# Cumulative sums in split fp32, keys by transposing, and square roots on ScalarE in three norms of a two-layer hybrid model

## The chip, the cores and the metric

One core of a Trainium2 chip runs the whole program. The metric is the device time of one execution in microseconds (us), of which the median over several runs is given. The engines are TensorE (PE in the profile; PEld is its weight load), VectorE (DVE), ScalarE (ACT), GpSimd (POOL) and SyncE (SP), whose queue issues most of the DMA transfers. Each engine works through its own queue in order and waits there on semaphores.

## The reference

The model has 256 tokens of width 1024 and two layers. Each layer is feed-forward, mixer, feed-forward, each with a root-mean-square norm ahead of it and a residual sum behind it; a last norm closes the program. The first layer's mixer joins retention and gated linear attention (GLA); the second one's joins a gated linear recurrence (RG-LRU) and an mLSTM. What the change touches, cut to its core:

```python
def rmsnorm(x, w):
    y = x * lax.rsqrt(jnp.mean(x * x, axis=-1, keepdims=True) + EPS)
    return y * w

# GLA: decay of every key channel, from a rank-16 projection, then sums over chunks of 64 tokens
log_a = jax.nn.log_sigmoid(glr @ w_lr_up + b_lr) / GLA_TAU      # 256x16 @ 16x256
b = jnp.cumsum(gc, axis=3)
b_mid = b[:, :, :, L // 2 - 1:L // 2]
s = einsum('bhnld,bhnsd->bhnls', qc * exp(b - b_mid), kc * exp(b_mid - b))
upd = einsum('bhnsd,bhnsv->nbhdv', kc * exp(b_end - b), vc)

# mLSTM: keys from the convolved and activated input
mc = silu(causal_dwconv(mu, ml_conv_w, ml_conv_b))
q = einsum('bshi,hij->bshj', mc, ml_wq)
k = einsum('bshi,hij->bshj', mc, ml_wk) * (ML_DH ** -0.5)
upd_c = einsum('bhns,bhnsd,bhnsv->nbhdv', w_end, kc, vc)

def swiglu(x, w_gu, w_down):
    g, u = split(x @ w_gu, 2, axis=-1)
    return (silu(g) * u) @ w_down
```

## The kernel before

The 256 tokens are two halves of 128, called t = 0 and t = 1 in the code; a half's tokens are the 128 partitions of a tile. All is fp32. A large product is taken as three products of a faster type (fp32r): `split` (L128) makes a high part (`hi`, ScalarE, L130) and the remainder (`lo`, VectorE, L131) of each operand, and `mm3` (L205) multiplies high by high (L209), low by high (L210) and high by low (L212) into one PSUM tile. A plain fp32 product is one instruction in the code and two on TensorE.

Units of work (a slice of a weight matrix with what is computed from it) are run in order, each for both halves, the second half lagging behind the first. Weights come as `raw` or `draw` tiles by DMA, and are split ahead of use. The feed-forward blocks combine some weight and activation slices by sums first (`draw`, formed on VectorE at L564; products at L547), so that seven products serve in place of eight. The small steps of the mixers (gates, convolutions, scans) run as side chains (`chain`, L186): each of their steps waits a number of ticks given in `STEPS`, and a tick is 512 columns of a large product on TensorE. So a side chain's matmuls fall between large products. Beyond that, a scheduler with a model of each engine orders the instructions of every engine, and `after` and `high_priority` bind some of them.

The places that the change touches:

- **The norms ahead of the feed-forward blocks** (`norm_f`, L332). ScalarE squares a half and sums it (L345, its sum read out behind it); GpSimd adds eps (L347) and raises to -0.5 (L348) to give `rs`; VectorE multiplies the half with the norm's weights (L349, `hs`) and then with `rs` (L352, two halves of 512 columns); TensorE transposes `hs` (L360) and the result is split (`Th`, `Tl`). The norms called f20, f11 and f21, ahead of the first layer's second block, the second layer's first and its second one, go this way; the first block's takes its root elsewhere.
- **GLA** (`gla_chain`, L794). The rank-16 gate input is transposed, multiplied by `w_lr_up` (tile `wlru`, L803), goes through a log-sigmoid (L738) to `la`, and is then summed over the tokens of a chunk in three ways by constant triangular matrices (`cum`, L811 to L813), with two columns of full sums (L815). The exponentials of these scale queries and keys.
- **mLSTM** (`ml_chain`, L1185). TensorE makes queries and keys from `mc` (L1195, L1196), channels on the partitions; ScalarE copies them out as `mqT` (L1199) and, scaled, `mkT` (L1200); TensorE makes the scores (L1204). For the first half the keys are needed once more with tokens on the partitions, for the state's update; TensorE multiplies `mc` by the key weights the other way round for it (L1212), and VectorE scales the result with the gate (L1215). The second half's chain begins with the convolution (ScalarE L1107, VectorE L1111) and a SiLU (L1189) that gives its `mc`.
- **The final norm** (`final_part`, L418). As above, by two halves of 512 columns; VectorE adds the two sums (L433), GpSimd raises to -0.5 (L434), VectorE scales 704 columns (L436) and ScalarE 320 (L437), and SyncE issues two stores (L439).

ScalarE holds one set of function tables at a time; where the next function needs another, an ACT_TABLE_LOAD stands ahead of it in the profile, with that function's line.

## Time and profile before

| | |
|---|---|
| median of 3 runs | 964.65 us (964.14 to 964.99) |
| profiled execution | 964.23 us, of which the span is 962.5 us |
| granted TensorE clock | 0.998 of full speed |
| instructions in the span | 11855 |
| table loads on ScalarE | 28, each 1.28 us |

The span runs from the first instruction to the last. A timeline row gives the start, the duration of the whole row, engine, line, operation, tiles (out<-in), shape, and with xN the number of instructions joined in it; a bracket names the idle time ahead of the row and what ended it. A group of instructions by line gives minimum, median and maximum in ns and the first and last start in us. Matmuls overlap, so their cost is read from one start to the next.

### The profile page before, as it was taken

The page shows a single profiled execution, that of the slowest core. Times are in us where ns is not written, and L with a number is a line of the kernel's source. Part 1 is how long each engine was busy: PE and PEld are TensorE (multiplying, and loading weights), DVE is VectorE, ACT ScalarE, POOL GpSimd, SP SyncE. Part 2 cuts the span into 40 slices and gives each one's busy share as a digit, 9 for nine tenths or more (in the row PEclk, how much of TensorE's full clock was granted, in tenths as well). Part 3 has the DMA queues.
Part 4 walks back from the last instruction along what each step waited for, and adds up shares of the span by engine and source line. Part 5 has one row for each costly group of instructions (what it writes and reads, how often), then busy time and mean ns, then how long its engine had stood idle before and what let it go on. Part 6 is the DMA issues. An engine that isn't in the chain of part 4 may idle for free.

```text
span 962.5 us, 11855 instructions
## 1 busy us (share of the span) xinstructions
PE 947.5 (98%) x4546; PEld 780.9 (81%) x4546; DVE 806.2 (84%) x932; ACT 602.5 (63%) x772; POOL 33.0 (3%) x60
## 2 busy tenths in 40 slices
...
DMA packets 105497, 180.86 MB, mean 188 GB/s; under 512 B 8196, under 2 KB 55200, under 8 KB 105440
## 3 DMA queue, kind: packets, MB, share of 16 engines
...
q8 instruction: 36, 0.59, 0.3%
q10 hardware_dynamic: 432, 0.55, 0.2%
q14 instruction: 21, 0.17, 0.0%
HBM read 179.03 MB, written 1.05 MB: 187 GB/s over the span
## 4 chain that ended last, share of the span: by engine, by line
PE 76%; DVE 11%; ACT 5%; issue 3%; DMA 3%; POOL 1%; SPq 0%; POOLq 0%; ACTq 0%; DVEq 0%
PE ps L547 20%; PE ps L209 9%; PE ps L212 9%; PE ps L210 9%; PE acc L209 8%; PE acc L212 8%; PE acc L210 8%; DVE lo L131 5%; DMA raw<-in_ffn_wgu_dram 2%; ACT hi L130 2%; DVE draw L564 1%; PE ps L574 1%; PE ps L226 1%; DVE mc L1111 1%; DMA draw<-in_ffn_wgu_dram 0%
## 5 line engine op out<-in xcount | busy, mean ns | idle before, releaser
L131 DVE TENSOR_TENSOR lo<-raw,hi 128x512 fp32r<-128x512 f32 (+4 forms) x222 | 301.8, 1382 | 51.8 <-ACT hi L130 51.0
L130 ACT ACTIVATE hi<-raw 128x512 fp32r<-128x512 f32 (+4 forms) x222 | 254.5, 1186 | 50.8 <-PE ps L212 25.5
L209 PE MATMUL ps<-hi,Th 128*128 128x512 f32 (+3 forms) x544 | 211.9, 390 | 0.2 <-ACT hi L130 0.2
L210 PE MATMUL ps<-lo,Th 128*128 128x512 f32 (+3 forms) x544 | 206.0, 379 | 2.2 <-DVE lo L131 2.2
L212 PE MATMUL ps<-hi,Tl 128*128 128x512 f32 (+3 forms) x544 | 205.9, 379 | 0.0
L131 DVE TENSOR_TENSOR lo<-draw,hi 128x2048 fp32r<-128x2048 f32 x72 | 164.1, 2285 | 10.2 <-ACT hi L130 9.8
L130 ACT ACTIVATE hi<-draw 128x2048 fp32r<-128x2048 f32 x72 | 137.8, 1916 | 38.8 <-DVE draw L564 25.7
L209 PE MATMUL acc<-hi,aT 128*128 128x512 f32 x352 | 138.9, 395 | 0.0
L210 PE MATMUL acc<-lo,aT 128*128 128x512 f32 x352 | 137.0, 390 | 0.0
L210 PEld LDWEIGHTS ps<-lo,Th 128*128 128x128 f32 x544 | 102.5, 188 | 21.2 <-DVE lo L131 4.2
L212 PEld LDWEIGHTS ps<-hi,Tl 128*128 128x128 f32 x544 | 102.2, 188 | 19.0
L209 PEld LDWEIGHTS ps<-hi,Th 128*128 128x128 f32 x544 | 102.2, 188 | 18.9 <-issue 1.4
L212 PE MATMUL acc<-hi,aT 128*128 128x512 f32 x352 | 109.6, 390 | 0.0
L564 DVE TENSOR_TENSOR draw<-draw,draw 128x2048 f32<-128x2048 f32 x36 | 81.9, 2283 | 3.8 <-DVE lo L131 2.7
L130 ACT ACTIVATE aT<-ps 128x256 fp32r<-128x256 f32 x88 | 32.8, 379 | 78.3 <-PE ps L226 51.2
L212 PEld LDWEIGHTS acc<-hi,aT 128*128 128x128 f32 x352 | 66.1, 188 | 13.9
L209 PEld LDWEIGHTS acc<-hi,aT 128*128 128x128 f32 x352 | 66.1, 188 | 13.1
L210 PEld LDWEIGHTS acc<-lo,aT 128*128 128x128 f32 x352 | 66.2, 188 | 13.0
L547 PE MATMUL ps<-hi,Th 128*128 128x512 f32 x144 | 57.0, 396 | 0.4 <-ACT hi L130 0.3
L547 PE MATMUL ps<-lo,Th 128*128 128x512 f32 x144 | 56.2, 390 | 0.8 <-DVE lo L131 0.8
L547 PE MATMUL ps<-hi,Tl 128*128 128x512 f32 x144 | 56.2, 390 | 0.0
L131 DVE TENSOR_TENSOR aT<-ps,aT 128x256 fp32r<-128x256 f32 x88 | 36.4, 418 | 18.8 <-ACT aT L130 18.6
...
## 6 DMA issues: line engine op xcount, KB each, us to landing
...
```

The costliest lines, as they stand in the source:

```text
L130: S.activation(hi2, src2, AF.Copy)
L131: V.tensor_tensor(out=lo2, in0=src2, in1=hi2.bitcast(F32), op=ALU.subtract)
L209: T.matmul(ps, xh[:, k, :], wk[0][:, sl], start=start, stop=False)
L210: T.matmul(ps, xh[:, k, :], wk[1][:, sl], start=False, stop=False)
L212: state["mm"] = T.matmul(ps, xl[:, k, :], wk[0][:, sl], start=False, stop=stop)
L226: T.transpose(pt[:, i * P:(i + 1) * P], src[:, i * P:(i + 1) * P], ident)
L547: state["mm"] = T.matmul(ps, x[a][:, k, :], w[b][:, k, :], start=first and k == 0 and i == 0, stop=k == 3 and i == 2, skip_group_check=not ...
L564: state["dve"] = V.tensor_tensor(out=out, in0=a, in1=b, op=op)
L574: T.transpose(pt[:, i * P:(i + 1) * P], a[:, i * P:(i + 1) * P], ident)
L1111: V.scalar_tensor_tensor(out=dst[:, g, :], in0=cb[:, g, o - 3 + i:o - 3 + i + P], scalar=cw[:, g, i:i + 1], in1=dst[:, g, :], op0=ALU.mult ...
```

## The change

- GLA: `w_lr_up` and the transposed gate are split, and their product becomes three fp32r products. `la` is split, and each of the three cumulative sums becomes two fp32r products, since the entries of the constant matrices are exact in fp32r; the two columns of full sums stay fp32. The constants come in two transfers, and ScalarE copies the larger. One entry of `STEPS`, the delay ahead of the sums, goes from 5 to 8.
- mLSTM, first half: the keys with tokens on the partitions come from transposing `mkT`, which is scaled already.
- Norms f20, f11, f21, first half: ScalarE takes the square root of mean plus eps, VectorE the reciprocal. A square root of a constant one into the same tile is placed after the large product last issued, at high priority. Second half: ScalarE adds eps, GpSimd takes the power as before.
- Final norm: ScalarE takes the root of the two sums' total (one sum as its bias), VectorE the reciprocal; the store of 320 columns goes to ScalarE's queue.

```diff
@@ -43,7 +43,7 @@
 TRP = 10
 NT = 2
 NTF = 10
-STEPS = (2, 2, 10, 5, 3, 3, 6, 7, 3, 1, 1, 30, 10, 10, 9, 8, 3, 2, 10, 3, 3, 2, 9, 2)
+STEPS = (2, 2, 10, 8, 3, 3, 6, 7, 3, 1, 1, 30, 10, 10, 9, 8, 3, 2, 10, 3, 3, 2, 9, 2)
 
 CUT = 320
 
@@ -123,6 +123,9 @@
 
     mh4 = cpool.tile([P, 4], F32, tag="mh4", name="mh4")
     G.memset(mh4, -0.5)
+
+    eps = cpool.tile([P, 1], F32, tag="eps", name="eps")
+    G.memset(eps, EPS)
 
 
     def split(src2, hi2, lo2):
@@ -342,10 +345,18 @@
             if not scaled:
                 ms = apool.tile([P, 1], F32, tag="ms", bufs=2, name=nm("ms"))
                 junk = apool.tile([P, D], BF16, tag="junk", bufs=1, name=nm("junk"))
+                rs = apool.tile([P, 1], F32, tag="rs1", bufs=4, name=nm("rs"))
+                if t == 0:
+
+                    with after(state["mm"]):
+                        S.activation(rs, one, AF.Sqrt)
                 S.activation(junk, h[t], AF.Square, scale=D ** -0.5, accum_out=ms)
-                rs = apool.tile([P, 1], F32, tag="rs1", bufs=4, name=nm("rs"))
-                G.tensor_scalar(out=ms, in0=ms, scalar1=EPS, scalar2=None, op0=ALU.add)
-                G.tensor_tensor(out=rs, in0=ms, in1=mh4[:, 0:1], op=ALU.pow)
+                if t == 0:
+                    S.activation(rs, ms, AF.Sqrt, bias=eps, scale=1.0)
+                    V.reciprocal(out=rs, in_=rs)
+                else:
+                    S.activation(ms, ms, AF.Identity, bias=eps, scale=1.0)
+                    G.tensor_tensor(out=rs, in0=ms, in1=mh4[:, 0:1], op=ALU.pow)
             V.tensor_tensor(out=hs, in0=h[t], in1=wB, op=ALU.mult)
             for n in range(2):
                 sl = slice(n * 512, n * 512 + 512)
@@ -430,13 +441,14 @@
             V.tensor_scalar(out=ms[:, 0:1], in0=ms[:, 0:1], scalar1=EPS, scalar2=None, op0=ALU.add)
             return
         rs = mt("frs", [P, 1], 2)
-        V.tensor_tensor(out=ms[:, 1:2], in0=ms[:, 1:2], in1=ms[:, 0:1], op=ALU.add)
-        G.tensor_tensor(out=rs, in0=ms[:, 1:2], in1=mh4[:, 0:1], op=ALU.pow)
+
+        S.activation(rs, ms[:, 1:2], AF.Sqrt, bias=ms[:, 0:1], scale=1.0)
+        V.reciprocal(out=rs, in_=rs)
         a, b = slice(0, CUT), slice(CUT, D)
         V.tensor_scalar(out=o[:, b], in0=hw[:, b], scalar1=rs, scalar2=None, op0=ALU.mult)
         S.activation(o[:, a], hw[:, a], AF.Copy, scale=rs)
-        for x in (b, a):
-            nc.sync.dma_start(out[0, t * P:(t + 1) * P, x], o[:, x])
+        nc.sync.dma_start(out[0, t * P:(t + 1) * P, b], o[:, b])
+        nc.scalar.dma_start(out[0, t * P:(t + 1) * P, a], o[:, a])
 
 
     def ffn_units(wgu, wd, nxt, layer0=False):
@@ -772,9 +784,17 @@
         def pre():
             open_pool("even")
             C["tri"] = const("tri", I["c_tri"], [P, P])
-            C["lrup"] = mconst("wlru", w_lr_up, [16, 256])
+            up = mt("rb", [16, 256])
+            nc.sync.dma_start(up, w_lr_up)
+            C["lrup"] = mt("lruh", [16, 256], 1, F32R), mt("lrul", [16, 256], 1, F32R)
+            split(up, *C["lrup"])
             C["blr"] = mconst("blr", brow(b_lr), [P, 256])
-            C["cum"] = mconst("cum", I["c_cum"], [P, 3 * P + 2])
+            C["cum"] = mconst("cum", I["c_cum"][:, 3 * P:], [P, 2])
+
+            cum = mt("sq", [P, 3 * P], 1)
+            nc.sync.dma_start(cum, I["c_cum"][:, :3 * P])
+            C["cumr"] = mt("cumr", [P, 3 * P], 1, F32R)
+            S.activation(C["cumr"], cum, AF.Copy)
             C["gmask"] = mconst("gmask", I["c_gmask"], [P, 2 * P], I32)
             for t in range(2):
                 load_rope(t, 0)
@@ -796,23 +816,28 @@
             yield STEPS[0]
             pt = ps_tile(tag="acc")
             T.transpose(pt[:16, :P], gl, ident)
-            glT = mt("glT", [16, P])
-            V.tensor_copy(glT, pt[:16, :P])
+            glT = mt("glTh", [16, P], 1, F32R), mt("glTl", [16, P], 1, F32R)
+            split(pt[:16, :P], *glT)
             yield STEPS[1]
             pz = ps_tile(tag="acc")
-            T.matmul(pz[:, :256], glT, C["lrup"], start=True, stop=True)
+            for i, (a, b) in enumerate(((0, 0), (0, 1), (1, 0))):
+                T.matmul(pz[:, :256], glT[a], C["lrup"][b], start=i == 0, stop=i == 2)
             la = mt("gz", [P, 256])
             V.tensor_tensor(out=la, in0=pz[:, :256], in1=C["blr"], op=ALU.add)
             logsigmoid(la, la, "g", 256)
+            lhl = mt("ge", [P, 256], 1, F32R), mt("E4", [P, 256], 1, F32R)
+            split(la, *lhl)
             yield STEPS[2]
 
             pb = ps_tile(tag="acc")
             pe = ps_tile(tag="acc")
-            T.matmul(pb[:, :256], C["cum"][:, 0:P], la, start=True, stop=True)
-            T.matmul(pb[:, 256:], C["cum"][:, P:2 * P], la, start=True, stop=True)
-            T.matmul(pe[:, :256], C["cum"][:, 2 * P:3 * P], la, start=True, stop=True)
+            last = None
+            for n, dst in enumerate((pb[:, :256], pb[:, 256:], pe[:, :256])):
+                for i in range(2):
+                    with after(last):
+                        last = T.matmul(dst, C["cumr"][:, n * P:(n + 1) * P], lhl[i], start=i == 0, stop=i == 1)
             for p in range(2):
-                T.matmul(pe[:, 256 + 2 * p:258 + 2 * p], la[:, p * P:(p + 1) * P], C["cum"][:, 3 * P:3 * P + 2],
+                T.matmul(pe[:, 256 + 2 * p:258 + 2 * p], la[:, p * P:(p + 1) * P], C["cum"],
                          start=True, stop=True)
             E1 = mt("E1", [P, 256])
             E2 = mt("E2", [P, 256])
@@ -1207,13 +1232,11 @@
             Sw = mt("mSw", [P, 4, P], 1)
             V.tensor_tensor(out=f2(Sw), in0=psS, in1=f2(E), op=ALU.mult)
             if t == 0:
-                pk2 = ps_tile(tag="acc")
-                for hd in range(4):
-                    T.matmul(pk2[:, hd * P:(hd + 1) * P], mc[:, hd, :], C["wqk"][:, 1, hd, :], start=True, stop=True)
+                pk2 = transposes(f2(kT), 4)
                 kw = mt("mkw", [P, 4, P])
                 for hd in range(4):
                     V.tensor_scalar(out=kw[:, hd, :], in0=pk2[:, hd * P:(hd + 1) * P], scalar1=E[:, hd, P - 1:P],
-                                    scalar2=sc, op0=ALU.mult, op1=ALU.mult)
+                                    scalar2=None, op0=ALU.mult)
             else:
 
                 yield has(t, "wi")
```

How the order of the instructions changes, at the three places of which the prediction speaks. First TensorE at the cumulative sums of the first half (`gz` is `la`; `ge` and `E_309` are its high and low part). A row of the order is one instruction of the code.

Before:

```order
L811 MATMUL acc_1737<-gz_1644,cum_1376 128x256
L812 MATMUL acc_1737<-gz_1644,cum_1376 128x256
L813 MATMUL acc_1738<-gz_1644,cum_1376 128x256
L815 MATMUL acc_1738<-cum_1376,gz_1644 128x2 x2
L308 MATMUL ps_1754<-ident,h_72 128x128
```

Now:

```order
L838 MATMUL acc_1755<-ge_1665,cumr_1386 128x256
L838 MATMUL acc_1755<-E_309_1666,cumr_1386 128x256
L838 MATMUL acc_1755<-ge_1665,cumr_1386 128x256
L838 MATMUL acc_1755<-E_309_1666,cumr_1386 128x256
L838 MATMUL acc_1756<-ge_1665,cumr_1386 128x256
L838 MATMUL acc_1756<-E_309_1666,cumr_1386 128x256
L840 MATMUL acc_1756<-cum_1382,gz_1658 128x2 x2
L311 MATMUL ps_1775<-ident,h_72 128x128
```

The block stands at the same place, between the same large products and ahead of the second half's transposes.

Second, VectorE at the second half's norm f21, ahead of the last feed-forward block: `h` is the residual stream (the mixer's output is added to it), `lo` the remainders of weights of the next products.

Before:

```order
L131 TENSOR_TENSOR lo_6672<-raw_6668,hi_6671 128x1024
L131 TENSOR_TENSOR lo_6681<-raw_6677,hi_6680 128x1024
L732 TENSOR_TENSOR h_72<-acc_6537,h_72 128x512
L732 TENSOR_TENSOR h_72<-acc_6538,h_72 128x512
L131 TENSOR_TENSOR lo_6681<-raw_6677,hi_6680 128x1024
L349 TENSOR_TENSOR hs_6609<-h_72,wB 128x1024
L131 TENSOR_TENSOR lo_6840<-draw_6837,hi_6839 128x2048
L352 TENSOR_SCALAR hs_6609<-hs_6609,rs_6613 128x512 x2
L564 TENSOR_TENSOR draw_6858<-draw_6858,draw_6837 128x2048
```

Now:

```order
L134 TENSOR_TENSOR lo_6707<-raw_6703,hi_6706 128x1024
L744 TENSOR_TENSOR h_72<-acc_6572,h_72 128x512
L744 TENSOR_TENSOR h_72<-acc_6573,h_72 128x512
L134 TENSOR_TENSOR lo_6716<-raw_6712,hi_6715 128x1024
L360 TENSOR_TENSOR hs_6644<-h_72,wB 128x1024
L134 TENSOR_TENSOR lo_6716<-raw_6712,hi_6715 128x1024
L363 TENSOR_SCALAR hs_6644<-hs_6644,rs_6647 128x512 x2
L134 TENSOR_TENSOR lo_6875<-draw_6872,hi_6874 128x2048
```

The subtraction of 2048 columns has moved from ahead of the scaling (L352, now L363) to behind it, and one of 1024 columns stands in its place. At f20, ahead of the first layer's second block, it is the other way round: a subtraction of 2048 columns now stands ahead of the scaling, and one of 1024 did before.

Third, ScalarE in the odd mixer, at the first half's mLSTM chain.

Before:

```order
L1199 COPY mqT_5790<-acc_5780 128x512
L1200 ACTIVATE mkT_5791<-acc_5781 128x512
L1171 ACT_TABLE_LOAD
L1171 ACTIVATE guard_5807<-acc_5805 128x4
L130 ACTIVATE hi_5910<-raw_5908 128x1024
L1107 ACTIVATE xc_5821<-lrucb_5320,lrucw_5318 128x128 x4
```

Now:

```order
L1224 COPY mqT_5824<-acc_5814 128x512
L352 ACT_TABLE_LOAD
L352 ACTIVATE rs_6564<-one 128x1
L1225 ACTIVATE mkT_5825<-acc_5815 128x512
L1196 ACT_TABLE_LOAD
L1196 ACTIVATE guard_5841<-acc_5839 128x4
L1132 ACTIVATE xc_5855<-lrucb_5354,lrucw_5352 128x128 x4
```

The constant's square root of norm f21, with its table load, has come in between `mqT` and `mkT`, and the weight conversion that stood ahead of `xc` has gone behind it.

## The prediction

> **What bounds the kernel now.** I read the totals first, then the chain that ended last, then the gaps in TensorE's timeline.
>
> ```profile
> PE 947.5 (98%) x4546; PEld 780.9 (81%) x4546; DVE 806.2 (84%) x932; ACT 602.5 (63%) x772; POOL 33.0 (3%) x60
> ```
>
> ```profile
> PE 76%; DVE 11%; ACT 5%; issue 3%; DMA 3%; POOL 1%; SPq 0%; POOLq 0%; ACTq 0%; DVEq 0%
> ```
>
> TensorE is busy nearly throughout, and three quarters of the chain are matmuls. So two things pay: TensorE time removed where it runs without a gap, and a gap closed. Work on VectorE, ScalarE or GpSimd counts only where TensorE waits for it, or after its last matmul. The profiled execution took 964.23 us; the median of the runs is 964.65, 0.42 more. I sum against the first and carry the difference over. This measurement can tell a change from none above about 0.2%, 1.9 us.
>
> **Cumulative sums: -1.14.** TensorE's timeline at the first of the two chains, then the group over both, then short split products elsewhere:
>
> ```profile
> 201.33 0.39 PE L212 MATMUL ps<-hi,Tl 128*128 128x512 f32 x1
> 201.56 0.59 PE L811 MATMUL acc<-gz,cum 128*128 128x256 f32 x2
> ...
> 202.85 0.50 PE L815 MATMUL acc<-cum,gz 128*128 128x2 f32 x4
> ```
>
> ```profile
> L811 PE MATMUL acc<-gz,cum x4: 377/377/378, 201.6 to 226.1; 128*128 128x256 f32 x4
> ```
>
> ```profile
> 194.93 0.28 PE L209 MATMUL ps<-hi,Th 128*128 128x256 f32 x1
> 195.05 0.28 PE L210 MATMUL ps<-lo,Th 128*128 128x256 f32 x1
> ```
>
> I count start to start, since matmuls overlap. Three fp32 products take six instructions and 202.85 - 201.56 = 1.29 us. A split product of 256 columns starts every 0.12, so the six new ones take 0.72. That is 0.57 less, twice 1.14. The matmuls stand back to back there, so it is time of the span. The new split ahead of the sums (a ScalarE and a VectorE instruction) costs TensorE nothing: the delay counter ahead of them goes from 5 to 8 ticks, and a tick is 512 columns of other products. Nor do the two splits of the gate's operands, the constants' extra copy, their two smaller loads on SyncE (issued long before use), and two further table loads that the first early root brings into these chains: TensorE has no gap in this stage that the work of the other engines ends, so they have room. If that cover is gone, the first to wait is the sum itself. Bounds: -0.9 to -1.2.
>
> **Rank-16 product: -0.2.**
>
> ```profile
> 193.84 0.69 PE L803 MATMUL acc<-wlru,glT 16*128 16x256 f32 x2
> 194.47 0.39 PE L209 MATMUL ps<-hi,Th 128*128 128x256 f32 x1
> ```
>
> Two instructions take 0.63 (194.47 - 193.84). No row shows a split product with 16 rows. At the full-height 0.12 each, three take 0.36: 0.27 less. With the extra that these two show over the full-height fp32 ones above (0.63 / 2 = 0.315 against 1.29 / 6 = 0.215, so 0.1 each) they take 0.66: nothing saved. Between 0 and -0.27 I take -0.1 for each of the two chains, nearer the row that has 16 rows.
>
> **Keys: -0.4 of TensorE time.**
>
> ```profile
> 696.80 1.05 PE L1212 MATMUL acc<-wqk,mc 128*128 128x128 f32 x8
> 697.61 0.36 PE L209 MATMUL ps<-hi,Th 128*128 128x256 f32 x1
> ```
>
> ```profile
> 772.21 0.60 PE L360 MATMUL ps<-ident,hs 128*128 128x128 f32 x4
> 772.64 0.38 PE L360 MATMUL acc<-ident,hs 128*128 128x128 f32 x2
> ```
>
> Eight instructions take 0.81; four transposes take 0.43. They now wait for ScalarE's mkT instead of for nothing new; the score product ahead of them in TensorE's queue needs mkT as well, so nothing behind them waits longer. Bounds: -0.4 to 0, if a later wait takes it up.
>
> **Second half's norm ahead of the last feed-forward block: -0.8.** TensorE, VectorE, then GpSimd:
>
> ```profile
> 783.78 0.39 PE L212 MATMUL ps<-hi,Tl 128*128 128x512 f32 x1
> 784.82 0.66 PE L360 MATMUL ps<-ident,hs 128*128 128x128 f32 x4 [0.65 <-DVE hs L352]
> ```
>
> ```profile
> 781.21 2.29 DVE L131 TENSOR_TENSOR lo<-draw,hi 128x2048 fp32r<-128x2048 f32 x1
> ```
>
> ```profile
> 780.57 3.01 POOL L347 TENSOR_SCALAR ms<-ms 128x1 f32<-128x1 f32 x1 [10.53 <-ACT junk L345]
> 783.66 0.58 POOL L348 TENSOR_TENSOR rs<-ms,mh 128x1 f32<-128x1 f32 x1
> ```
>
> A one-column addition takes 3.01 us on GpSimd, and ends 0.08 after VectorE's long subtraction (781.21 + 2.29 = 783.50). The power follows, then the scaling, and TensorE starts 1.04 after its last matmul where 0.23 is usual: 0.81 lost. Afterwards ScalarE adds eps, so one GpSimd step is gone. More important, the order now puts a 1024-column subtraction (1.2 us) there, and the 2048-column one behind the scaling. If the power is shut out until that shorter one ends (781.21 + 1.22 = 782.43), plus 0.43 (next part), the scaling starts near 782.9 and its first half is done near 783.4; TensorE comes for it at 783.78 + 0.23 = 784.01. I take the whole gap, -0.8; the other end is 0.
>
> The Trainium skill, page SBUF — State Buffer, section "SBUF: two separate sides", says that VectorE operations with two SBUF inputs and GpSimd share a port pair as an exclusive lock, held for a whole instruction. The two rows above agree; by it the change gains here through the shorter subtraction and not through the missing addition.
>
> **Second half's norm ahead of the first layer's second block: +0.2.** GpSimd, VectorE, TensorE:
>
> ```profile
> 321.30 1.41 POOL L348 TENSOR_TENSOR rs<-ms,mh 128x1 f32<-128x1 f32 x1
> ```
>
> ```profile
> 321.06 1.22 DVE L131 TENSOR_TENSOR lo<-raw,hi 128x1024 fp32r<-128x1024 f32 x1
> 322.75 0.49 DVE L352 TENSOR_SCALAR hs<-hs,rs 128x512 f32<-128x512 f32 x1 [0.47 <-POOL rs L348]
> ```
>
> ```profile
> 323.74 0.49 PE L360 MATMUL ps<-ident,hs 128*128 128x128 f32 x3
> ```
>
> Here the order changes the wrong way: a 2048-column subtraction (2.29) takes the place of the 1024-column one (1.22) at 321.06 and ends at 323.35. The power ended 0.43 after its subtraction (322.28); shut out again, it ends at 323.78, and the first half of the scaling (0.49) at 324.3. TensorE is there at 323.74 + 0.23 = 323.97, since one matmul moved ahead. So nearly 0.4 is lost, or nothing if the power slips in before the long one. I take 0.2. After the root's table ScalarE must load the SiLU table again, which it didn't here; it has 2.35 us of idle time for it:
>
> ```profile
> 322.57 0.38 ACT L468 ACTIVATE ffs<-ps 128x256 f32<-128x256 f32 x1 [2.35 <-PE ps L212]
> ```
>
> **First half's norms: 0.** ScalarE does one conversion, loads the Sqrt table, takes the root; VectorE inverts:
>
> ```profile
> 308.05 2.01 ACT L130 ACTIVATE hi<-raw 128x1024 fp32r<-128x1024 f32 x2 [0.19 <-PE acc L212]
> ```
>
> ```profile
> 311.95 0.60 PE L360 MATMUL ps<-ident,hs 128*128 128x128 f32 x4
> ```
>
> ```profile
> 705.50 0.30 ACT L743 ACTIVATE fe<-fe,one 128x4 f32<-128x4 f32 x1
> ```
>
> ```profile
> L1254 DVE RECIPROCAL den<-den x4: 156/166/167, 719.7 to 742.8; 128x2 f32<-128x2 f32 x4
> ```
>
> From 308.05: one conversion 1.04, load 1.28 (row below), root 0.30 (a small activation with a bias column), reciprocal 0.17, half a scaling 0.49, and 0.15 of hand-overs: 311.5, and TensorE comes at 311.95. In the last block ScalarE's conversion starts at 768.97:
>
> ```profile
> 768.97 1.99 ACT L130 ACTIVATE hi<-raw 128x1024 fp32r<-128x1024 f32 x2
> ```
>
> The same 3.4 us give 772.4; TensorE came at 772.21, but three matmuls moved ahead, so 772.89. Both have about 0.5 to spare. The third such norm, at the second layer's start, has no conversion ahead of the load and more room. VectorE's reciprocal is a new wait for ScalarE; behind it in its queue stand the scaling and weight subtractions, and a 2.3 us form (L564) was moved out from behind them, so TensorE's next block finds them done. Bounds: 0 to +1.0, if a further conversion of 1.0 slips ahead of each load.
>
> **The early Sqrt in the odd mixer: +0.6.** A root of a constant, which would load the table ahead of the norm at 769, stands between mqT and mkT, some 75 us before it; other functions follow, so the load at the norm remains. The rows there, and the first half's block that waits later:
>
> ```profile
> 692.67 0.60 ACT L1200 ACTIVATE mkT<-acc 128x512 f32<-128x512 f32 x1
> 693.30 1.28 ACT L1171 ACT_TABLE_LOAD   x1
> 694.59 0.17 ACT L1171 ACTIVATE guard<-acc 128x4 f32<-128x4 f32 x1
> 695.61 1.64 ACT L1107 ACTIVATE xc<-lrucb,lrucw 128x128 f32<-128x128 f32 x4
> ```
>
> ```profile
> 715.85 0.49 PE L1195 MATMUL acc<-mc,wqk 128*128 128x128 f32 x2 [0.61 <-ACT mc L1189]
> ```
>
> ScalarE has 1.28 + 0.17 = 1.45 more to do before mkT, and TensorE later waits for ScalarE's mc. Behind mkT stand xc, the gates and mc; VectorE's convolution waits for xc. A conversion of 1.05 that stood before xc now stands behind, so xc is only 0.4 to 0.6 late; but that conversion and its subtraction are then late in turn. On TensorE five more 512-column matmuls (1.1 us) now stand ahead of the block that uses mc, the keys' 0.4 fewer, so it comes there 0.7 later. Ends: -0.6 (the present wait covered) and +1.5 (all 1.45 paid). I take +0.6, as other waits of this stage may grow too.
>
> The Trainium skill, page ScalarE: Activation LUTs, section "What ACT_TABLE_LOAD costs", prices a switch at a 1283 ns load plus a drain of about 1380 ns. This trace has the load but no drain: it starts 0.03 behind mkT's end and the next activation 0.01 behind its own. By the page the sum would be some 3 us worse.
>
> **The end: -0.6.**
>
> ```profile
> 957.41 0.16 DVE L433 TENSOR_TENSOR ms<-ms 128x1 f32<-128x1 f32 x1
> 957.65 0.55 POOL L434 TENSOR_TENSOR frs<-ms,mh 128x1 f32<-128x1 f32 x1 [7.55 <-DVE ms L433]
> 958.23 0.56 ACT L437 ACTIVATE fo<-hw,frs 128x320 f32<-128x320 f32 x1 [0.85 <-POOL frs L434]
> 958.23 0.59 DVE L436 TENSOR_SCALAR fo<-hw,frs 128x704 f32<-128x704 f32 x1 [0.66 <-POOL frs L434]
> 958.82 0.81 SPq L439 DMA_DIRECT2D out_dram<-fo  x2
> ```
>
> Everything here sets the end. Addition and power take 0.82 with their hand-overs (958.23 - 957.41); root 0.30, reciprocal 0.17 and two hand-overs of 0.04 take 0.55: 0.27 less. The two stores were issued one behind the other on SyncE in 0.81; now the second is on ScalarE's queue, so the later starts up to 0.4 earlier. I take -0.6: -0.3 if the second queue brings nothing, -0.7 at most. The Sqrt table was loaded for the first half's root, whose power ran over 7 us earlier (the bracket at 957.65).
>
> **Sum.** -1.14 - 0.2 - 0.4 - 0.8 + 0.2 + 0 + 0.6 - 0.6 = -2.34: 961.9 profiled, **962.3** as a median.
>
> **Rivals.**
> - *The odd mixer takes it back*: the 1.45 on ScalarE reaches mc in full and the keys' 0.4 is only waited longer. Against it, the moved matmuls. +0.9 and +0.4 on the forecast: 963.6. Chance 0.2.
> - *The change doesn't do what it says at the norms*: GpSimd stays shut out in both second halves, the gap at 783.78 remains. For it, the 3.01 and 1.41 us rows. +0.8 + 0.2: 963.3. Chance 0.1.
> - *A table switch costs twice its row*: a drain as long as the load, at the two tight norms (1.28 - 0.5 each) and in the odd mixer (1.28): +2.8, 965.1. Against it, the 0.01 and 0.03 us around the load. Chance 0.05.
> - *Slower, by the early Sqrt in the odd mixer*: ScalarE is 1.45 late and VectorE idles about 1.0 for xc with its subtractions queued behind. It decides from the point where TensorE pays this 2.45 in both halves' chains, not once: 2 x 2.45 - 0.6 = +4.3, with the norms' spare lost a little more: 967. For it, ScalarE runs gapless around that load. Against it, the halves' chains overlap in time, so a delay is paid once. Chance 0.1.
>
> **How the numbers follow.** My forecast has 0.5, and spans 960.6 to 963.0; a larger gain (rank-16 products, stores) another 0.05. Faster means under 962.7: 0.45 of the forecast's 0.5, all of the larger gain, 0.03 of the rivals: 0.53. Slower means over 966.6: 0.1. The same: 0.37. The range takes in the first three rivals, 960.5 to 965.2, and leaves out the slower case and a little below.
>
> **What would show it.** Six sums about 0.12 apart; TensorE's last L360 group 0.23 after its matmul instead of 1.04, with the GpSimd addition's 3.01 gone; no TensorE wait at the first halves' norms; its wait for mc at most 1.5 us; the reciprocal of the last norm 0.35 behind ScalarE's root's start, and two stores that start together. A wait above 2 us for mc, or a new one at 311 or 772, would make me wrong.

## The result and the profile after

| | before | changed kernel |
|---|---|---|
| median (22 runs each, on the same chips) | 964.22 us (963.21 to 965.11) | 965.54 us (964.80 to 969.05) |
| profiled execution, its span | 964.23, 962.5 us | 964.80, 963.0 us |
| table loads on ScalarE | 28 | 39 |

The ratio is 1.0018, with a 95% interval of 1.0012 to 1.0023: 1.3 us slower at the medians, where 2.3 us faster was forecast. 965.54 lies outside the range. It is 0.18%, so by the bound set ahead it counts as no change, though the interval leaves out 1. One execution of e13 below took 3928.8 us and one of e14 5445.07; without these two their medians are 965.48 and 963.03, and differences in the text use those.

The page of the changed kernel, its first line on engines (busy time, share, instructions) and its shares of the chain:

```profile
PE 946.3 (98%) x4544; PEld 779.4 (81%) x4544; DVE 807.7 (84%) x938; ACT 616.6 (64%) x798; POOL 29.2 (3%) x50
```

```profile
PE 77%; DVE 10%; ACT 7%; DMA 3%; issue 2%; POOL 0%; SPq 0%; DVEq 0%; ACTq 0%; POOLq 0%
```

TensorE's busy sum fell by 1.2 us and ScalarE's rose by 14.1, about what the eleven more table loads take (11 x 1.28). On the chain ScalarE's share rose from 5% to 7%, TensorE's from 76% to 77%, and those of VectorE, GpSimd and issue fell by one point each. Where time went is read by cutting the span at the starts of TensorE rows that every version has: the first row of the rank-16 product, of f20's transposes for each half, of the first half's mLSTM queries, of f21's transposes for the second half, and the last matmul. "End" runs from the last matmul's start to the end of the span. Times in us, each from one profiled execution; the experiments below are in the table as well.

| kernel | start | GLA | f20 | to odd mixer | odd mixer | last block | end | span | median |
|---|---|---|---|---|---|---|---|---|---|
| before | 193.84 | 118.10 | 11.79 | 366.69 | 94.38 | 170.63 | 7.01 | 962.46 | 964.22 |
| changed | 192.36 | 118.57 | 12.28 | 366.54 | 95.42 | 170.81 | 7.03 | 963.02 | 965.54 |
| e1_no_early_root | 192.33 | 117.42 | 12.28 | 366.46 | 96.23 | 170.78 | 7.03 | 962.53 | 965.94 |
| e2_gla_only | 193.28 | 117.26 | 11.79 | 366.89 | 95.48 | 170.76 | 7.45 | 962.90 | 964.42 |
| e3_norms_only | 192.80 | 118.14 | 12.29 | 366.35 | 97.68 | 170.81 | 6.97 | 965.04 | 965.43 |
| e4_tail_only | 193.18 | 118.12 | 11.79 | 366.84 | 94.53 | 170.65 | 6.88 | 961.99 | 963.87 |
| e5_gla_one_load | 192.86 | 117.28 | 11.79 | 367.03 | 94.55 | 170.63 | 7.01 | 961.16 | 963.03 |
| e6_norms_no_early | 193.33 | 118.14 | 12.29 | 366.48 | 94.08 | 170.83 | 6.99 | 962.14 | 964.00 |
| e7_norms_second_only | 193.33 | 118.14 | 11.77 | 366.78 | 94.50 | 170.77 | 6.98 | 962.27 | 964.04 |
| e8_keys_only | 192.75 | 118.09 | 11.79 | 367.16 | 96.76 | 170.85 | 7.01 | 964.40 | 967.26 |
| e9_keys_twice | 194.28 | 118.08 | 11.79 | 366.84 | 94.57 | 170.63 | 7.01 | 963.20 | 964.36 |
| e10_keys_later | 192.97 | 118.08 | 11.79 | 367.18 | 94.79 | 172.08 | 7.01 | 963.90 | 964.43 |
| e11_repaired | 194.25 | 117.44 | 12.28 | 366.58 | 94.17 | 170.78 | 6.81 | 962.32 | 963.52 |
| e12_best | 193.76 | 117.36 | 11.77 | 367.14 | 94.63 | 170.80 | 6.68 | 962.14 | 963.18 |
| e13_without_keys | 192.80 | 118.56 | 12.28 | 366.42 | 94.99 | 170.83 | 7.03 | 962.90 | 965.67 |
| e14_gla_root | 193.45 | 117.30 | 11.79 | 366.63 | 95.23 | 170.63 | 6.72 | 961.75 | 963.05 |
| e15_gla_root_last | 193.73 | 117.38 | 11.77 | 367.12 | 93.96 | 170.81 | 6.68 | 961.46 | 962.79 |
| e16_root_f21 | 192.77 | 117.39 | 12.29 | 366.50 | 94.76 | 170.81 | 7.03 | 961.55 | 964.29 |
| e17_root_not_f21 | 192.65 | 118.53 | 12.29 | 366.45 | 94.09 | 170.79 | 7.04 | 961.82 | 965.40 |

The first stage holds nothing that e4, e8, e9 and e10 edit, and yet it takes 192.75 to 194.28 in them and 193.84 before. In e9, as in e11, TensorE's clock fell to half for 3.41 us at 25 us (last section), which is 1.7 of that; the other four still differ by 1.1. So two spans can't be compared to better than that; GLA, f20 and the end can, since they agree to some 0.05 in kernels that leave them alone. The odd mixer's stage too differs between kernels that leave it as it was: 94.38 before, e5 94.55, e14 95.23, and e2 95.48, as much as the changed kernel. Changed less before, without the start: +0.47 in GLA, +0.49 at f20, -0.15, +1.04 in the odd mixer, +0.18, +0.02 at the end; together +2.05 (the medians say +1.32). The profiled execution needn't be a typical one: that of the changed kernel is the fastest of its 22, e17's of its 11, 1.8 below the median.

**GLA: two new waits.** TensorE's waits of the changed kernel between 190 and 310 us (total, times, longest); before, this list is empty:

```profile
PE acc L894 <- DVE gS L882: 0.5, 1, 0.5
PE acc L879 <- DVE gqkT L868: 0.5, 1, 0.5
```

What stands ahead of the second is read in the timelines of ScalarE, VectorE and TensorE of the changed kernel:

```profile
207.33 1.28 ACT L352 ACT_TABLE_LOAD   x1
208.62 0.20 ACT L352 ACTIVATE rs<-one 128x1 f32<-128x1 f32 x1
208.73 0.67 ACT L942 ACTIVATE gv<-ps,rs 128x512 f32<-128x512 f32 x1
209.31 1.14 ACT L133 ACTIVATE hi<-raw 128x512 fp32r<-128x512 f32 x2
```

```profile
209.96 1.29 DVE L134 TENSOR_TENSOR lo<-raw,hi 128x512 fp32r<-128x512 f32 x2 [1.96 <-ACT hi L133]
211.17 0.68 DVE L868 COPY gqkT<-acc 128x512 f32<-128x512 f32 x1
```

```profile
211.91 0.49 PE L879 MATMUL acc<-gqkT 64*128 64x128 f32 x4 [0.50 <-DVE gqkT L868]
```

f20's early root and its table load hold ScalarE from 207.33 to 208.73. The conversion `hi` behind them is late, VectorE idles 1.96 us for it, and the copy of `gqkT`, which needs nothing from ScalarE, stands in VectorE's queue behind the two subtractions that do. TensorE comes for it 0.5 us too early. `gS` stands behind four more such subtractions. It takes two edits together: in e2, with GLA's edits and no early root, the queue has this order but VectorE idles only 0.52 us there; in e3, with the early root alone, the copy stands ahead of the subtractions, as before. Neither kernel has these waits. It was wrong to ask only whether ScalarE has spare time in the stage: the delay passed through a queue to something else.

**Odd mixer.** ScalarE's timeline of the changed kernel, and TensorE's waits between 690 and 790 us:

```profile
692.11 1.28 ACT L352 ACT_TABLE_LOAD   x1
693.40 0.20 ACT L352 ACTIVATE rs<-one 128x1 f32<-128x1 f32 x1
693.51 0.58 ACT L1225 ACTIVATE mkT<-acc 128x512 f32<-128x512 f32 x1
...
695.47 1.64 ACT L1132 ACTIVATE xc<-lrucb,lrucw 128x128 f32<-128x128 f32 x4
```

```profile
PE ps L213 <- DVE lo L134: 1.7, 2, 1.4
PE acc L212 <- ACT Th L133: 0.6, 1, 0.6
```

The stage starts at 690.43 before and 689.76 now. From there, `mkT` is 1.51 late and `xc` 0.53 late (5.18 before, 5.71 now), as forecast. The wait for `mc` is gone, and so is the 0.6 us for `hs`; in their place TensorE waits for weights (`lo`) and, at 765.82, for the high part of the RG-LRU branch's output (`Th`, from `lh`) at the output product. The wait for `lo` is followed up with e16 and e17.

### The profile page after: what moved, and what is told of

The parts are those of the page before. It is cut to its first block, busy times and chain, and to the rows that moved or that the text cites. A ratio compares the mean times of both kernels' runs of the same rounds, so it can differ in the third digit from the quotient of the medians.

```text
span 963.0 us, 11858 instructions
## 1 busy us (share of the span) xinstructions
PE 946.3 (98%) x4544; PEld 779.4 (81%) x4544; DVE 807.7 (84%) x938; ACT 616.6 (64%) x798; POOL 29.2 (3%) x50
## 4 chain that ended last, share of the span: by engine, by line
PE 77%; DVE 10%; ACT 7%; DMA 3%; issue 2%; POOL 0%; SPq 0%; DVEq 0%; ACTq 0%; POOLq 0%
PE ps L559 20%; PE ps L212 9%; PE ps L213 9%; PE ps L215 9%; PE acc L212 8%; PE acc L213 8%; PE acc L215 8%; DVE lo L134 5%; ACT hi L133 3%; DMA raw<-in_ffn_wgu_dram 2%; DVE draw L576 1%; PE ps L586 1%; PE ps L229 1%; DMA r<-mx 1%; ACT Th L243 1%
```

## Experiments: the parts alone

Each experiment was timed in eleven executions (e8 in eight, e13 in twelve) beside the kernel before on the same chip; a ratio is to that.

**e1, the changed kernel without the early root.**

```diff
-                if t == 0:
-                    with after(state["mm"]):
-                        S.activation(rs, one, AF.Sqrt)
```

> The changed kernel without the square root of the constant one in the three norms (a computation whose result is overwritten, so nothing of the output is left out). Theory A, the early root is what takes the savings: in the changed kernel TensorE waits 0.55 us for gqkT and 0.49 us for gS in the GLA chain, behind a table load of 1.28 us that stands there, and the odd mixer is 2.2 us longer. Without it both go: about 3 us less than the changed kernel's 965.5, so 962.0 to 963.0. Rival B, the odd mixer is longer because the keys' transposes and the other edits reorder it: only the GLA waits go, about 1 us, 964.3 to 964.8. Rival C, the Sqrt loads at the norms themselves: no change, 965.5.

Measured: 965.94 against 964.14, ratio 1.0015 (1.0006 to 1.0024), as slow as with the root: as rival C has it, but not for its reason, since the stages moved: GLA fell by 1.15, to 117.42, and the odd mixer rose by 0.8, to 96.23. Something that the early root had hidden came up there: TensorE's waits are of the kinds of e8 (`Th` 1.2, `hi` 0.7, `hm` 0.7, `lo` 0.6; in e8 1.2, 0.7, 0.6 and 1.0).

**e2, GLA's edits alone** (products, splits, two transfers, the delay of 8).

```diff
+            C["cum"] = mconst("cum", I["c_cum"][:, 3 * P:], [P, 2])
+            cum = mt("sq", [P, 3 * P], 1)
+            nc.sync.dma_start(cum, I["c_cum"][:, :3 * P])
...
+                        last = T.matmul(dst, C["cumr"][:, n * P:(n + 1) * P], lhl[i], start=i == 0, stop=i == 1)
```

> The kernel before with the GLA part alone (split rank-16 product, split sums, delay 8 instead of 5). If the matmuls saved are time of the span, as the prediction put it: -1.14 for the sums and -0.2 to -0.3 for the rank-16 product, ratio 0.9984 to 0.9987, about 962.8 against 964.2. If the extra splits on ScalarE and VectorE bring new waits in that stage, or a later stage takes it back: within 0.3 us of the kernel before.

Measured: 964.42 against 964.14, ratio 1.0001 (0.9992 to 1.0010). GLA's stage does gain 0.84, so the sums' gain is real; the end is 0.43 longer, although nothing at the end was edited.

**e3, the three norms alone, with the early root.**

```diff
+                    with after(state["mm"]):
+                        S.activation(rs, one, AF.Sqrt)
...
+                if t == 0:
+                    S.activation(rs, ms, AF.Sqrt, bias=eps, scale=1.0)
+                    V.reciprocal(out=rs, in_=rs)
+                else:
+                    S.activation(ms, ms, AF.Identity, bias=eps, scale=1.0)
```

> The kernel before with the three norms' part alone, the early root included. Theory A (the early root costs about 1 in the GLA chain and up to 2.2 in the odd mixer, the norm of the last block gains 0.8, the one of the first layer's second block loses 0.2 to 0.3): +1.5 to +2.7 us, 965.7 to 966.9. Rival B (the odd mixer's 2.2 come from the keys and the reordering): +0.3 to +0.6, 964.5 to 964.8.

Measured: 965.43 against 964.14, ratio 1.0017 (1.0008 to 1.0025): the norms alone are as slow as the whole change, but not in the same places. GLA's stage is as before (118.14): the root's place does no harm where VectorE keeps the old order.

**e4, the final norm alone.**

```diff
+        S.activation(rs, ms[:, 1:2], AF.Sqrt, bias=ms[:, 0:1], scale=1.0)
+        V.reciprocal(out=rs, in_=rs)
...
+        nc.scalar.dma_start(out[0, t * P:(t + 1) * P, a], o[:, a])
```

> The kernel before with the final norm's part alone. The trace of the changed kernel shows the root and the reciprocal 0.30 us shorter than the addition and the power, the last store landed 0.12 us sooner after the scaling, and then eight waits of SyncE on the DMA queues, 0.06 us each, that come after the landing instead of before it (0.43 us). Theory T, these waits eat the gain: within 0.1 us of the kernel before. The prediction's own: -0.6 us.

Measured: 963.87 against 964.14, ratio 0.9999 (0.9991 to 1.0008). The end is 6.88 for 7.01: -0.13 where -0.6 was forecast.

## Experiments: which piece of each part

**e5, GLA with the constants in one transfer.**

```diff
-            C["cum"] = mconst("cum", I["c_cum"][:, 3 * P:], [P, 2])
-            cum = mt("sq", [P, 3 * P], 1)
-            nc.sync.dma_start(cum, I["c_cum"][:, :3 * P])
+            cum = mt("sq", [P, 3 * P + 2], 1)
+            nc.sync.dma_start(cum, I["c_cum"])
+            C["cum"] = mt("cum", [P, 2], 1)
+            V.tensor_copy(C["cum"], cum[:, 3 * P:])
```

> The GLA part alone, but with its constants in one transfer instead of two (VectorE copies the two fp32 columns out). The GLA part alone was even with the kernel before although its trace is 0.85 us shorter from the rank-16 product to the next norm. Theory L: its one extra transfer turns the round of the eight DMA queues, so that SyncE's end waits begin with the last store's queue and seven more waits (0.44 us) follow the landing; and the gate's round trip through DRAM in the odd mixer eats part of the rest. With one transfer the 0.44 us come back: 963.1 to 963.7, 0.4 to 0.5 under the GLA part alone. Rival: the end waits don't matter, it stays at 964.1 to 964.5.

Measured: 963.03 against 964.31, ratio 0.9991 (0.9982 to 1.0000). GLA keeps its gain (117.28) and the end is back at 7.01. TensorE's timeline at the rank-16 product and the sums:

```profile
192.86 0.39 PE L812 MATMUL acc<-lruh,glTh 16*128 16x256 f32 x1
...
193.42 0.38 PE L209 MATMUL ps<-hi,Th 128*128 128x256 f32 x1
```

```profile
200.50 0.28 PE L826 MATMUL acc<-ge,cumr 128*128 128x256 f32 x1
...
201.25 0.50 PE L828 MATMUL acc<-cum,gz 128*128 128x2 f32 x4
```

Six sums take 0.75 (1.29 before), the product 0.56 (0.63 before): -0.54 and -0.07 per half, -1.22 in all. The stage shows -0.82. Of the rest, 0.18 is a wait for `rk` at 265.44 that wasn't there before; the other 0.2 stands under no wait that the trace tells.

The end is explained by SyncE's waits there, of before and of e2 (total, times, longest):

```profile
SPq L1474 <- DMA out_dram<-fo: 1.5, 2, 0.9
```

```profile
SPq L1487 <- DMA out_dram<-fo: 1.9, 1, 1.9
```

At the end of each of these programs SyncE waits in turn for eight DMA queues, in the same order, some 0.06 us each. Transfers are dealt round the queues, so one transfer more turns the round by one. In the kernel before, the store that lands last is on the queue asked for last: SyncE's last wait ends at 961.57 and it goes on at 961.63. In e2 that store is on the queue asked for first, and seven more waits follow (961.57 to 962.08). The split transfer so costs e2 0.43 us at the far end of the program. In the changed kernel it is SyncE's own store that is asked for first; it lands 0.17 us ahead of ScalarE's, and the seven waits run from 961.70 to 962.20. There the turn costs less: its end is 7.03, with the same two stores it is 6.88 in e4 and 6.81 in e11.

**e6, e3 without the early root** (the same three lines removed as in e1).

> The kernel before with the norms' part alone and without the early root. With the early root it was 1.3 us slower than the kernel before. Theory A': the early root's 1.45 us on ScalarE in the odd mixer are most of it; without it 963.5 to 964.4. Rival B': the first half's roots at the norms reorder the program (the 2048-column subtraction ahead of the scaling at two norms, 0.5 and 0.2 us; other places in the odd mixer): still 965.0 to 966.0, with the trace's waits at f20 and f11 as in the changed kernel.

Measured: 964.00 against 964.31, ratio 0.9995 (0.9986 to 1.0004), 1.6 below e3 (each taken against its own kernel before). The odd mixer's stage is 94.08 against e3's 97.68; the other stages behind the start are equal to 0.2. Of that difference about 1.7 is a fall of TensorE's clock in e3's profiled execution (last section), and 1.9 is left.

**e7, the second halves' norms alone** (the first halves stay on GpSimd).

```diff
+                if t == 0:
+                    G.tensor_scalar(out=ms, in0=ms, scalar1=EPS, scalar2=None, op0=ALU.add)
+                else:
+                    S.activation(ms, ms, AF.Identity, bias=eps, scale=1.0)
```

> The kernel before with only the second half's norms changed (ScalarE adds eps, GpSimd takes the power). The order on VectorE stays that of before, with the 2048-column subtraction ahead of the scaling at the last block's norm. If the port decides, the power is shut out to 783.5 in place of the addition and ends 0.43 later: the scaling starts about 0.3 us sooner, -0.3 us. If the addition was the cost, the whole gap of 0.81 goes: -0.8 us. Rival: no change, under 0.2 us.

Measured: 964.04 against 964.31, ratio 0.9999 (0.9990 to 1.0008). Taking GpSimd's addition away gains nothing in the median. In the trace it gains what the first theory said, 0.3: TensorE starts f21's transposes 0.73 after its last matmul (784.52 after 783.79; 1.04 before), and other small waits of the odd mixer take it up. f20's stage is 11.77: the 0.5 us at f20 comes with the new order of VectorE, which this kernel doesn't have.

**e8, the transposed keys alone.**

```diff
-                pk2 = ps_tile(tag="acc")
-                for hd in range(4):
-                    T.matmul(pk2[:, hd * P:(hd + 1) * P], mc[:, hd, :], C["wqk"][:, 1, hd, :], start=True, stop=True)
+                pk2 = transposes(f2(kT), 4)
```

> The kernel before with the keys' transposes alone. Prediction's step: 0.4 us of TensorE time saved, of the span unless a later wait takes it up. Its order also has a 1024-column subtraction instead of the 2048-column one ahead of the last block's scaling, so if that order gives the 0.8 us and not the norm's change, this kernel gains them too: -0.8 to -1.2 us. If the odd mixer's waits are set by other chains (the gate's round trip through DRAM), the keys' 0.4 are only waited: -0.8 at most, 0 if both fail.

Measured: 967.26 against 964.31, ratio 1.0029 (1.0019 to 1.0039): 3.0 us slower, the most of any kernel here, by an edit that takes 0.4 us off TensorE. TensorE's waits of e8 between 690 and 790 us:

```profile
PE acc L209 <- ACT Th L130: 1.2, 1, 1.2
PE ps L210 <- DVE lo L131: 1.0, 1, 1.0
```

These are its two longest, and none of its waits is for the keys. The scheduler works on modelled times, and with four transposes for eight instructions it arranges the 70 us behind them differently on TensorE, VectorE and ScalarE. VectorE's order just behind (`mSw` and `mkw` are the scores and keys with the gate):

```diff
+L1208 TENSOR_TENSOR mSw_5860<-acc_5849,mE_5803 128x512
+L1213 TENSOR_SCALAR mkw_5867<-acc_5862,mE_5803 128x128 x4
 L741 SCALAR_TENSOR_TENSOR fe_5875<-g_1101_5872 128x4
-L131 TENSOR_TENSOR lo_5919<-raw_5916,hi_5918 128x1024
-L1208 TENSOR_TENSOR mSw_5860<-acc_5849,mE_5803 128x512
-L1215 TENSOR_SCALAR mkw_5867<-acc_5862,mE_5803 128x128 x4
```

The new order also has the 1024-column subtraction ahead of f21's scaling, with GpSimd's addition still there, and TensorE loses nothing at that place:

```profile
786.31 0.40 PE L212 MATMUL ps<-hi,Tl 128*128 128x512 f32 x1
786.54 0.60 PE L360 MATMUL ps<-ident,hs 128*128 128x128 f32 x4
```

**e9, the keys with each transpose done twice**, so that the scheduler sees eight instructions as before.

```diff
-        for i in range(n):
+        for i in [i for i in range(n) for _ in range(rep)]:
...
+                pk2 = transposes(f2(kT), 4, rep=2)
```

> The keys' transposes alone, but each done twice into the same place, so that TensorE works on them about as long (8 of 0.11 us) as on the product that they replace (0.81 us). On VectorE and ScalarE the instructions then stand in the order of before, on TensorE too but for the replaced ones. The keys alone took 3.0 us more than the kernel before, with 4.6 us of TensorE waits in the second half of the odd mixer against 1. Theory O, the new order of the odd mixer costs it, and not the transposes: within 0.3 us of the kernel before, 964.0 to 964.6. Rival D, the new dependence on ScalarE's mkT costs it: still 966 to 967.

Measured: 964.36 against 964.24, ratio 0.9999 (0.9990 to 1.0008). The keys come from the transposes as in e8, the order is that of before, and the 3.0 us are gone: they were the order's, not the transposes'.

**e10, the keys with one delay of the side chains longer**, which nearly restores the order.

```diff
-STEPS = (2, 2, 10, 5, 3, 3, 6, 7, 3, 1, 1, 30, 10, 10, 9, 8, 3, 2, 10, 3, 3, 2, 9, 2)
+STEPS = (2, 2, 10, 5, 3, 3, 6, 7, 3, 1, 1, 30, 10, 10, 9, 8, 3, 2, 10, 4, 3, 2, 9, 2)
```

> The keys' transposes alone, with one delay counter of the mLSTM chain at 4 ticks instead of 3, which brings the order back (all but two instructions on VectorE and ScalarE, 21 on TensorE). Theory O: the waits of the second half go, 964.0 to 964.4, and up to 0.4 less if the TensorE time saved counts, 963.6. Rival D: 966 to 967. If even an order close to the old one is enough to lose, more than 965.

Measured: 964.43 against 964.24, ratio 1.0001 (0.9992 to 1.0010). Without the cost of the order, the keys' 0.4 us still doesn't show. The odd mixer is at 94.79; its profiled execution is 1.4 us longer in the last block and stands 1.3 above its own median. There ScalarE idles 3.81 us, up to 874.42, for a late transfer of down-projection weights (0.88 before), and TensorE then waits 1.28 us at 879.41 for a `cs` that stands in VectorE's queue behind these weights' subtraction.

## Experiments: putting it together

**e11, the changed kernel repaired**: no early root, one transfer, the delay of e10.

> The changed kernel with three repairs: no early root, the sums' constants in one transfer, one delay counter of the mLSTM chain at 4 ticks instead of 3. By the parts: GLA with one transfer -1.3 (measured), norms without the early root -0.3 (measured), final norm -0.1 to -0.3 (measured -0.27 with an interval around 0), keys 0 to -0.4: 962.0 to 962.8, if theory O holds and the parts add up. If the transposes themselves lose, or the parts don't add up, 964 or more.

Measured: 963.52 against 964.24, ratio 0.9990 (0.9981 to 0.9999), 2.0 below the changed kernel.

**e12, the pieces that had gained**: GLA with one transfer, the final root with both stores on SyncE, the keys with the delay of e10, and the new norm at f21 only, without the early root.

```diff
-            norm_f(t)
+            norm_f(t, alt=name == "f21")
...
+        S.activation(rs, ms[:, 1:2], AF.Sqrt, bias=ms[:, 0:1], scale=1.0)
+        V.reciprocal(out=rs, in_=rs)
```

> The GLA part with one transfer, the final norm's root on ScalarE with both stores on SyncE as before, the keys' transposes with the longer delay, and the changed norm at the last block only, without the early root. The norms at f20 and f11, whose order lost 0.5 and 0.2 us, stay as before. By the parts -1.3 (GLA), -0.3 (root), -0.8 (last block's gap), 0 to -0.4 (keys): 961.5 to 962.2. If the odd mixer's waits take it up, 963 or more.

Measured: 963.18 against 964.24, ratio 0.9988 (0.9979 to 0.9997). f20's stage is as before, the end 6.68.

**e13, the changed kernel with the fp32 key product of before.**

```diff
-                pk2 = transposes(f2(kT), 4)
+                pk2 = ps_tile(tag="acc")
+                for hd in range(4):
+                    T.matmul(pk2[:, hd * P:(hd + 1) * P], mc[:, hd, :], C["wqk"][:, 1, hd, :], start=True, stop=True)
```

> The changed kernel without the keys' part (the fp32 product stays), early root and all else as in the change. On ScalarE and VectorE its instructions stand in the changed kernel's order but for one. Theory E, in the changed kernel the early root alone makes the odd mixer longer and the keys change nothing: 965.2 to 966.0. Rival K, the keys' reordering costs in the changed kernel as it does alone: 963 to 964.

Measured: 965.67 against 964.05, ratio 1.0016 (1.0007 to 1.0025), as the changed kernel. With the early root in place the keys neither cost nor gain: the new order of e8 doesn't arise then.

**e14, GLA with one transfer and the final root, stores on SyncE.** The diffs are those of e5 and, of e4, the root without the second queue.

> The GLA part with one transfer and the final norm's root on ScalarE, both stores on SyncE as before; no keys, no other norms. By the parts: 1.3 from GLA and 0.3 from the root, 962.6 to 962.9. If the gain doesn't add up: 963.0 or more.

Measured: 963.05 against 964.05, ratio 0.9989 (0.9980 to 0.9997). The end is 6.72, 0.17 shorter than e4's with its two queues.

**e15, e14 and the new norm at f21 without the early root** (the diff of e12 at `norm_f`).

> As e14, with the last block's norm changed too (first half's root on ScalarE, no early root). The gap of 0.8 us at its second half goes, but the versions e11 and e12 that have this show 1.1 us more of waits at 764 to 766, ahead of it. If those waits come from the changed norm: no gain over e14, within 0.3. If they come from the keys' later delay: 0.8 under e14, 961.8 to 962.1.

Measured: 962.79 against 964.05, ratio 0.9991 (0.9982 to 0.9999). It has the lowest median, and the shortest odd mixer, 93.96. e5, e11, e12, e14 and e15 are all about 0.1% faster than the kernel before (e5's interval ends at 1.0000), and no run here ranks them.

**e16 and e17, the early roots apart**, both on the base of e13. e16 keeps only f21's, e17 only those of f20 and f11.

```diff
-                if t == 0:
+                if t == 0 and early:
...
-            norm_f(t)
+            norm_f(t, early=name == "f21")
```

> The changed kernel with the fp32 key product, in which only norm f21 keeps its early square root of a constant; those of f20 and f11 are gone. The theory that each early root costs where it lands, two times apart: the GLA stage loses its two waits (118.56 to 117.4 us between the rank-16 product and the first half's transposes of f20), while the odd mixer keeps the table load between mqT and mkT, so its stage stays near 95.0 us or above, the SyncE row with the two transfers of the odd mixer's output weights stays 4.2 us long (it is 3.5 in every kernel without this root), and the gate's round trip through DRAM (from GpSimd's store of mx to VectorE's use of mE, second half) stays at 9.4 us. Median about 1.1 below the kernel with all early roots, 964.5. The rival, that the odd mixer's stage varies by chance between programs: stage 94.0 to 94.5, row 3.5, round trip 8.2 to 8.8, median 963.8.

> The opposite half: the changed kernel with the fp32 key product, f20 and f11 keep their early roots, f21 has none. The theory that each early root costs where it lands: the GLA stage keeps 118.5 us and its two waits, the odd mixer's stage comes down to 94.0 to 94.4 us with the SyncE row at 3.5 and the round trip at 8.2 to 8.8 us; median 0.8 to 1.6 below the kernel with all early roots, near 964.3. The rival, that the odd mixer's stage varies by chance: stage 95 again and median 965.3 or more.

Measured: e16 964.29 against 964.11, ratio 1.0002 (0.9993 to 1.0011); e17 965.40, ratio 1.0012 (1.0003 to 1.0021). The stages follow where the root is: GLA 117.39 without f20's and 118.53 with it, the odd mixer 94.76 with f21's and 94.09 without. The longest of TensorE's waits in the odd mixer of e17 is that for `mc` again (0.6), as before.

The medians agree for the root in GLA: without it (and f11's, whose stage doesn't move) 1.25 comes off (e13 is 1.43 above its kernel before, e16 0.18), and TensorE's order is the same in both kernels. For the odd mixer's they don't: e17, expected near 964.3, is only 0.1 below e13 by the same reckoning (its stage 0.9), where e6 is 1.6 below e3. Their intervals are some 0.9 us to each side, and without f21's root TensorE's order differs too, so the price of that root is left at 0.1 to 1.6.

What it does there can be read. The second half's gate makes a round trip through DRAM: GpSimd stores `mx`, loads `mE` back, VectorE uses it. Timelines of GpSimd and VectorE, of before and of the changed kernel, and the `lo` for which TensorE waits:

```profile
724.98 0.54 POOL L1126 DMA_DIRECT2D r<-mx  x1 [3.62 <-DVE mx L1153]
733.25 1.14 DVE L1175 SCALAR_TENSOR_TENSOR mE<-mE,ab,big 128x128 f32<-128x128 f32 x4 [0.88 <-DMA mE<-r]
```

```profile
724.51 0.54 POOL L1151 DMA_DIRECT2D r<-mx  x1 [3.17 <-DVE mx L1178]
733.90 1.14 DVE L1200 SCALAR_TENSOR_TENSOR mE<-mE,ab,big 128x128 f32<-128x128 f32 x4 [1.88 <-DMA mE<-r]
...
736.15 1.21 DVE L134 TENSOR_TENSOR lo<-raw,hi 128x1024 fp32r<-128x1024 f32 x1
```

```profile
737.42 0.50 PE L213 MATMUL ps<-lo,Th 128*128 128x512 f32 x1 [1.35 <-DVE lo L134]
```

It is GLA's pattern again: VectorE idles for `mE`, and the subtraction that makes `lo`, which doesn't need `mE`, stands behind it in the queue. TensorE's wait follows VectorE's idle time from kernel to kernel. At 0.81 to 0.93 (before, e4, e5, e7, e9, e15) there is no such wait; at 1.18 (e14) it is 0.36, at 1.29 (e6) 0.47, at 1.33 (e17) 0.48, at 1.43 (e2) 0.63, at 1.76 (e16) 1.25, at 1.88 (changed) 1.35, at 2.43 (e3) 1.89. (e10 to e12, with the keys' longer delay, wait 0.47 to 0.58 at 0.84 to 0.94.) This is part of why kernels that leave the odd mixer alone, as e2, differ there.

The round trip takes 8.27 before and 9.39 in the changed kernel; with f21's early root it is 9.3 to 9.9 (e16 9.26, e3 9.92), without it 8.2 to 8.8 (e4 8.20, e2 8.81), and 7.17 in e1 and e8, whose order is another and whose losses lie elsewhere. SyncE loads the output weights at the same time, in two transfers; the second is issued 0.67 later in each of the four kernels with the root (the two take 4.19 or 4.20 from first to last in the changed kernel, e3, e13 and e16, and 3.53 or 3.54 in before, e6, e10, e11, e12, e15 and e17). That the late megabyte stands in the way of the small load was not tried by itself.

## Why the prediction was wrong, by its steps

The forecast's terms sum to -2.34 against before; the medians moved by +1.32.

- **The cover of the sums: the step that failed most.** "two further table loads that the first early root brings into these chains: TensorE has no gap in this stage that the work of the other engines ends, so they have room". They had none: without the root the stage is 1.15 us (e1) and 1.17 us (e16) shorter, and the two waits above are gone. The sums and the rank-16 product themselves came out (-1.22 for -1.34); with the 0.4 lost behind them the stage would gain 0.84 (e2), and with the early root it loses 0.47. The text said that the sum itself would be the first to wait if the cover was gone. What waited was a copy queued behind late subtractions.
- **The end, -0.6: failed by its second half and by what comes after the stores.** The root did its part. The rows of the changed kernel's timeline, which stand in the order of time:

```profile
957.96 0.30 ACT L445 ACTIVATE frs<-ms 128x1 f32<-128x1 f32 x1
958.28 0.16 DVE L446 RECIPROCAL frs<-frs 128x1 f32<-128x1 f32 x1 [0.45 <-ACT frs L445]
...
958.48 0.59 DVE L448 TENSOR_SCALAR fo<-hw,frs 128x704 f32<-128x704 f32 x1
959.07 0.38 ACTq L451 DMA_DIRECT2D out_dram<-fo  x1
959.10 0.34 SPq L450 DMA_DIRECT2D out_dram<-fo  x1
```

  From the root's start to the scaling it takes 0.52 (0.55 forecast), and the two stores start together. That is 0.30 less than before. But stores that start together land no sooner: from the scaling's start to the last landing it takes 3.37 where it took 3.32. And from that landing to the end of the span it takes 1.17 where it took 0.91, since more of SyncE's waits, turned round by the constants' second transfer, come behind it. Net: +0.02.
- **Keys, -0.4: not gained.** The instructions are fewer, as forecast; nothing of it reached the end in e10, e9 or e13. The lower bound, 0, held. That the edit could move the order and cost 3.0 (e8) was no case of the prediction; in the changed kernel itself it doesn't happen.
- **The early Sqrt in the odd mixer, +0.6: right place, wrong wait, its size unsettled.** It is 0.1 by the medians of e17 and e13, 1.6 by those of e6 and e3, and the wait for `mc` that it rested on did not come: what came is the wait for `lo` behind the gate's round trip. The stage grew by 1.04 although it also holds f21's gain of 0.8. If the other misses keep their stage sizes (1.8 in GLA, 0.6 at the end, 0.4 keys, 0.1 at f20, 0.2 at f11), 0.6 of the 3.66 is left, and this term would be 1.2. The rival "slower, by the early Sqrt in the odd mixer" had the sign, but named 967 and one place; by e16 and e17 the larger part of the price lay in GLA (1.25 by the medians, 1.15 by the stage).
- **f20's second half, +0.2: right.** GpSimd, VectorE and TensorE of the changed kernel:

```profile
319.51 3.13 POOL L359 TENSOR_TENSOR rs<-ms,mh 128x1 f32<-128x1 f32 x1 [38.92 <-ACT ms L358]
```

```profile
319.94 2.28 DVE L134 TENSOR_TENSOR lo<-draw,hi 128x2048 fp32r<-128x2048 f32 x1
322.67 0.88 DVE L363 TENSOR_SCALAR hs<-hs,rs 128x512 f32<-128x512 f32 x2 [0.45 <-POOL rs L359]
```

```profile
322.70 0.39 PE L212 MATMUL ps<-hi,Th 128*128 128x512 f32 x1
323.21 0.66 PE L371 MATMUL ps<-ident,hs 128*128 128x128 f32 x4
```

  The power was shut out by the long subtraction and ended 0.42 behind it (319.51 + 3.13 = 322.64; 319.94 + 2.28 = 322.22), as worked out. TensorE starts 0.51 after its last matmul where 0.23 is usual: 0.28 lost. The rest of the stage's 0.49 is one matmul more in it. At f11's second half, for which the forecast had no term, a long subtraction shuts the power out in the same way and 0.22 is lost (502.57 after 502.12, where it was 503.37 after 503.14).
- **f21's second half, -0.8: right, and for the reason given.** The same three engines:

```profile
781.99 1.56 POOL L359 TENSOR_TENSOR rs<-ms,mh 128x1 f32<-128x1 f32 x1 [22.25 <-ACT ms L358]
```

```profile
781.91 1.22 DVE L134 TENSOR_TENSOR lo<-raw,hi 128x1024 fp32r<-128x1024 f32 x1
```

```profile
784.95 0.39 PE L215 MATMUL ps<-hi,Tl 128*128 128x512 f32 x1
785.18 0.60 PE L371 MATMUL ps<-ident,hs 128*128 128x128 f32 x4
```

  TensorE starts 0.23 after its last matmul; 1.04 before. The power, shut out again, ended 0.42 behind a subtraction that is now the shorter one. This is what the Trainium skill states on the page SBUF — State Buffer, section "SBUF: two separate sides": the shared port pair is held for a whole instruction. e8, with the new order and the addition still there, has the 0.23 as well; e7, without the addition and with the old order, keeps 0.73. So it is the order that gains here. The 0.8 is inside the odd mixer's stage, which grew all the same.
- **First halves' norms, 0: right.** ScalarE and TensorE of the changed kernel at f20:

```profile
308.11 1.28 ACT L355 ACT_TABLE_LOAD   x1
309.40 0.30 ACT L355 ACTIVATE rs<-ms,eps 128x1 f32<-128x1 f32 x1
```

```profile
310.93 0.60 PE L371 MATMUL ps<-ident,hs 128*128 128x128 f32 x4
```

  No bracket, so no wait, in spite of the load. The root starts 0.01 after the load's end, so no drain is seen here either, and the rival of a dearer table switch is out. It also shows that the early root bought nothing: the load at the norm remained, and had room. The price that the Trainium skill gives on the page ScalarE: Activation LUTs, section "What ACT_TABLE_LOAD costs", a drain on top of the load, is out for this trace as well.

What stays open: why the round trip through DRAM takes longer in some kernels; how much of the medians comes from falls of the clock (last section); which of the five faster versions is best; and why the single gains of e12 don't add up.
